# A decoder layer with 32 experts: experts of at most 64 tokens on unsplit float32 weights, one expert to a step

## Chip, core and metric

The kernel runs on one core of one Trainium2 chip. The metric is the device time of one execution in microseconds (us). Five engines work side by side, each through its own instructions in order: TensorE (PE, with PEld for its weight loads), VectorE (DVE), ScalarE (ACT), GpSimd (POOL) and SyncE (SP), which issues most transfers (DMAs).

## What is computed

The layer has 512 tokens of 1024 elements. Attention and a matrix memory come first; then each token goes to 4 of 32 experts. The change is in the experts alone:

```python
def expert_block(args):
    xb, eb = args
    up = jnp.dot(xb, w_up[eb]) + b_up[eb]              # 1024 -> 2048
    glu, lin = jnp.split(up, 2, axis=-1)
    glu = jnp.minimum(glu, SWIGLU_LIMIT)
    lin = jnp.clip(lin, -SWIGLU_LIMIT, SWIGLU_LIMIT)
    act = glu * jax.nn.sigmoid(SWIGLU_ALPHA * glu) * (lin + 1.0)
    return jnp.dot(act, w_down[eb]) + b_down[eb]       # 1024 -> 1024
```

Everything is float32. An expert's weights are 12 MB, so 384 MB are read for all of them.

## The kernel before

The first 440 us or so hold everything up to the routing. After that the experts run in steps. Weights come in tiles of 1 MB, [128, 2048] in SBUF: eight for an expert's up projection, four for its down projection, 384 in all. `rawtile` gives each the next of eight raw buffers (`NW`); `up_w` and `dn_w` issue its load on SP, which waits until that buffer is free.

`wsplit` makes two float32r tiles of a raw one: `whi`, the value rounded (an ACT copy, line 1111), and `wlo`, the rest (a DVE subtraction, line 1103). The tokens are split too (`tsplit`), and `mm_w` builds a product out of three: high by high, low by high, high by low. `parts` keeps four tiles ahead (`NS`): whichever tile PE works on, the splits of the next three already stand in the orders of ACT and DVE.

The experts are sorted by their number of tokens, and `KINDS` says what a step holds. S is one expert with up to 128 slots; a tile is 12 matmuls of 512 columns. X is the one with up to 192. H is a pair of experts with up to 64 slots each. In H, the stationary operand has the high parts of 64 tokens in one half of PE's columns and their low parts in the other, so that a tile is 8 matmuls; `low` copies the lower half of the result into the bias table `bt` and `comb` adds it to the upper half, with the bias.

A step's order is that of `tiles`: the up tiles of its expert with the down tiles of the step before in between. `after_tiles(n, f)` puts f behind the n-th tile that follows; the activation's transposes (`turn`), the gather's transposes (`turn_x`), the scatter of an expert's rows and the index computations (`prep`) are placed so. From step 2 on PE, ACT, DVE and POOL follow this order literally (`manual_schedule`). PSUM is four tiles: `uA` and `uB` for an up projection, `dn` for a down projection and `t` for all transposes.

Rows of tokens are gathered by an indirect DMA of POOL into the one buffer `xg0` (line 1117), and results scattered into `y4` in HBM (line 1296). After the last step the four rows of each token are loaded from `y4` (`partial`), weighted and summed on DVE, normalized and stored (`finish`). The last expert's result stays on chip and is added by matmuls (line 1672).

Of the kernel before, what the change touches and what calls it, by code (L numbers as in the profile page):

```python
# [9 lines left out]
F32 = mybir.dt.float32  # L10
# [29 lines left out]
SLOTS = {"S": (128,), "X": (192,), "H": (64, 64)}  # L40
KINDS = "SSHSSHSSHSXSHSSHSSHSHSHS"
# [3 lines left out]
def _steps():  # L45

    steps, caps = [], []
    for kd in KINDS:
        steps.append((SLOTS[kd], len(caps)))
        caps += SLOTS[kd]  # L50
    by = [*range(E0), *sorted(range(E0, E), key=lambda x: -caps[x])]
    assert len(caps) == E and KINDS.count("X") == 1 and KINDS[-1] == "S"
    return steps, [by.index(x) for x in range(E)], [caps[x] for x in by]
# [6 lines left out]
def _const_main():  # L60
# [7 lines left out]
    c[:, C_R:C_R + 32] = np.array(_steps()[1])[None]  # L68
# [52 lines left out]
def emit(tc, A, dbg=None, stop_at=99):  # L121
# [911 lines left out]


    bt = ep.tile([128, 3072], F32R, name="bt")
    sel = ep.tile([64, 2, 32], F32R, name="sel")
    for i in range(2):
        o = slice(32 * i, 32 * i + 32)
        nc.vector.tensor_copy(sel[o, 0], cst[o, C_ID + 32 * i:C_ID + 32 * i + 32])
    cmb = [ep.tile([128, 2, 64], F32R, name=f"cmb{i}") for i in range(2)]  # L1040
    for t in cmb:
        nc.vector.tensor_copy(t[64:128], cst[64:128, C_ID + 64:C_ID + 128][:, None, :].to_broadcast([64, 2, 64]))

    scat = []

    def bias_rows():
        up_, dn_ = A["b_up"][0], A["b_down"][0]
        for c, tg, src in ((0, "y", up_[:, 0:1024]), (1024, "l", up_[:, 1024:2048]), (2048, "y", dn_)):
            raw = ep.tile([64, 1024], F32, name=f"braw{c}", tag=tg)
            for r in (0, 32):  # L1050
                nc.gpsimd.dma_start(raw[r:r + 32], src)
            if c == 1024:
                nc.gpsimd.tensor_scalar(raw, raw, 1.0, 1.0, op0=OP.add, op1=OP.mult)
            o = bt[0:64, c:c + 1024]
            nc.scalar.activation(o, raw, AF.Copy)
            nc.gpsimd.tensor_tensor(o[32:64], raw[32:64], o[32:64].bitcast(F32), op=OP.subtract)

    def indices(sets, tag, late=False):
# [12 lines left out]

        def rest():
# [9 lines left out]
            return nc.vector.scalar_tensor_tensor(di, ti, 4.0, sv[:, :, 2], op0=OP.mult, op1=OP.add)  # L1082
        return ti, di, rest if late else rest()

    def half_w(src, c, k2):

        raw = rawtile([128, 2, 2, 512])
        for r in range(2):
            k.load(raw[:, r], src[(2 * k2 + r) * 128:(2 * k2 + r + 1) * 128, :].rearrange(
                "p (h c n) -> p h c n", h=2, c=2)[:, :, c, :])  # L1090
        return raw
# [6 lines left out]
    hold, los = [0], []  # L1098

    def lows():  # L1100
        while los and not hold[0]:
            lo, f, hi = los.pop(0)
            nc.vector.tensor_sub(lo, f, hi.bitcast(F32))  # L1103

    def wsplit(raw):

        nb[0] += 1
        f = raw if len(raw.shape) == 2 else raw.rearrange("p a n -> p (a n)") if len(raw.shape) == 3 else raw.rearrange(
            "p a b n -> p (a b n)")
# [14 lines left out]
    def tsplit(src, nm, kd=(128,), scale=None):  # L1124

# [3 lines left out]
        n = sum(kd)  # L1129
        pz = pq.tile([128, 8, n], F32, name=f"{nm}T{nb[0]}", tag="t")  # L1130
        for kk in range(KT):
            c = slice(kk * 128, (kk + 1) * 128) if nm == "x" else slice(kk // 2 * 256 + kk % 2, kk // 2 * 256 + kk % 2 + 255, 2)
            nc.tensor.transpose(pz[:, kk, :], src[:, c], ident[0:n, 0:n])  # L1133
        t = ep.tile([128, 8, 256], F32R, name=f"{nm}t{nb[0]}", tag=f"t{s_}")
        w = kd[0]
        v = t[:, :, 0:2 * n].rearrange("p k (e c s) -> p k e c s", c=2, s=w)
        if n == 2 * w:
            v = t.rearrange("p k (e c s) -> p (k e) c s", c=2, s=w)
            return t, k.split(v[:, :, 0], v[:, :, 1], pz.rearrange("p k (e s) -> p (k e) s", s=w), scale), s_
        return t, k.split(v[:, :, 0, 0], v[:, :, 0, 1], pz, scale), s_  # L1140
# [5 lines left out]
    def mm_w(outs, xT, kk, ws, first, j=None, last=False):  # L1146


        if j is not None:
            x = xT[0][:, kk, 128 * j:128 * j + 128]  # L1150
            for c in range(2):
                for o, w in zip(outs, ws):
                    nc.tensor.matmul(o, lhsT=x, rhs=w[c], start=first and c == 0, stop=last and c == 1)  # L1153
            return
# [8 lines left out]
    def mm_b(outs, sel_, c0):  # L1163
        for n, o in enumerate(outs):
            nc.tensor.matmul(o, lhsT=sel_.to_broadcast([64, 128]), rhs=bt[0:64, c0[n]:c0[n] + 512], start=False,
                             stop=True)

    def low(pt, c0):

        for h in range(2):  # L1170
            if c0[1] == c0[0] + 512:
# [39 lines left out]
    def etile(tag):  # L1211
        nb[0] += 1
        return ep.tile([128, D], F32, name=f"{tag}{nb[0]}", tag=tag)
# [532 lines left out]
```

## Time and profile before

| | us |
|---|---|
| median of 3 runs | 1611.37 (1611.22 to 1612.34) |
| the profiled execution's own time | 1610.24 |
| its span, first to last instruction | 1608.5 |
| PE busy | 1471.2 (91%) |
| DVE busy | 1351.0 (84%) |
| ACT busy | 1109.5 (69%) |
| POOL busy | 208.9 (13%) |
| bytes moved by DMA | 494.21 MB, mean 307 GB/s |

A share over the whole span mixes stages with different limits. In the profile's slices one digit is a fortieth of the span, 40.2 us. PE's busy time counts overlapping matmuls with modelled ends: how long PE needs for a matmul is read from the distance of two starts.

### The profile page before, as it was taken

Reading aid. Unit: us, or ns where it says so; the run is one execution under the profiler, and the core shown is the slowest. Engines: PE = TensorE matmul, PEld = TensorE weight load, DVE = VectorE, ACT = ScalarE, POOL = GpSimd, SP = SyncE. Lnnn points to the kernel's source line nnn. Section 1 sums busy time; section 2 is a strip of 40 time slices with the busy share of each in tenths; the row PEclk is TensorE's granted clock in tenths of the full one; section 3 lists DMA queues with packets and bytes.
Section 4 is the critical chain, followed back from the end, with each engine's and each line's share of the span. In section 5 each row is a group of like instructions: output and inputs, shape, how many; then the busy total and the mean of one; then the engine's idle time right before and its main releaser. Section 6 shows DMA issues by size and latency. Waiting matters only on the chain. (4 is left out here: it accounts for less than half of the span.)

```text
span 1608.5 us, 19732 instructions
## 1 busy us (share of the span) xinstructions
PE 1471.2 (91%) x6923; PEld 1121.7 (70%) x6923; DVE 1351.0 (84%) x1472; ACT 1109.5 (69%) x1071; POOL 208.9 (13%) x164
## 2 busy tenths in 40 slices
PE   7999999898679999999999999979999999999980
PEld 2888775676557678777777777758777777676760
DVE  2786737766878899999899676989999899999976
ACT  3555425564456888888698566958887888989951
POOL 0200100000450011021020010301022020110002
PEclk9999999999689999999999999989999999999995
DMA  8522257228387999999999777989999999999952
GB/s 293 168 70 79 67 173 263 101 89 303 136 320 286 344 419 408 404 404 420 367 415 402 298 294 276 395 331 379 372 415 418 351 413 403 420 419 418 417 241 97
DMA packets 104843, 494.21 MB, mean 307 GB/s; under 512 B 14330, under 2 KB 39395, under 8 KB 52643
## 3 DMA queue, kind: packets, MB, share of 16 engines
q1 hardware_dynamic: 96339, 472.12, 75.1%
q0 software_dynamic: 8400, 20.78, 3.6%
q8 instruction: 56, 0.92, 0.2%
q14 instruction: 48, 0.39, 0.1%
HBM read 474.77 MB, written 27.00 MB: 312 GB/s over the span
## 5 line engine op out<-in xcount | busy, mean ns | idle before, releaser
L1103 DVE TENSOR_TENSOR wlo<-raw,whi 128x2048 fp32r<-128x2048 f32 x384 | 861.2, 2294 | 51.4 <-ACT whi L1111 51.0
L1111 ACT ACTIVATE whi<-raw 128x2048 fp32r<-128x2048 f32 x384 | 719.0, 1911 | 80.0 <-PE dn L1153 28.0
L1117 POOL DMA_INDIRECT xg<-h2d,tis x25 | 70.1, 2806 | 571.4 <-PE xT L1133 563.5
L1296 POOL DMA_INDIRECT y<-y,dis x24 | 48.7, 2028 | 376.1 <-ACT y L1326 211.5
L1153 PE MATMUL ug<-wlo,xt 128*128 128x512 f32 x256 | 86.7, 420 | 10.8 <-DVE wlo L1103 7.1
L1153 PE MATMUL dn<-wlo,at 128*128 128x512 f32 x272 | 87.1, 401 | 1.8 <-DVE wlo L1103 1.4
L1153 PE MATMUL dn<-whi,at 128*128 128x512 f32 x272 | 88.4, 406 | 0.0
L1157 PE MATMUL dn<-whi,at 128*128 128x512 f32 x256 | 82.1, 402 | 1.2 <-ACT y L1335 1.2
L1153 PE MATMUL ug<-whi,xt 128*128 128x512 f32 x256 | 82.0, 401 | 1.3 <-ACT sg L1335 1.3
L1161 PE MATMUL dn<-wlo,at 128*128 128x512 f32 x256 | 81.9, 401 | 0.5
L1157 PE MATMUL ug<-whi,xt 128*128 128x512 f32 x240 | 80.4, 416 | 1.2 <-issue 1.2
L1159 PE MATMUL dn<-whi,at 128*128 128x512 f32 x256 | 80.9, 397 | 0.0
L1153 PE MATMUL ul<-whi,xt 128*128 128x512 f32 x256 | 80.4, 395 | 0.0
L1153 PE MATMUL ul<-wlo,xt 128*128 128x512 f32 x256 | 80.4, 395 | 0.0
L1157 PE MATMUL ul<-whi,xt 128*128 128x512 f32 x240 | 77.1, 403 | 1.6 <-DVE l L1208 1.5
L1159 PE MATMUL ul<-whi,xt 128*128 128x512 f32 x240 | 76.7, 400 | 0.0
L1159 PE MATMUL ug<-whi,xt 128*128 128x512 f32 x240 | 76.6, 401 | 0.0
L1161 PE MATMUL ug<-wlo,xt 128*128 128x512 f32 x240 | 76.0, 397 | 0.0
L1161 PE MATMUL ul<-wlo,xt 128*128 128x512 f32 x240 | 75.2, 394 | 0.0
L1153 PEld LDWEIGHTS ug<-wlo,xt 128*128 128x128 f32 x256 | 43.6, 189 | 42.2 <-DVE wlo L1103 36.1
L1153 PEld LDWEIGHTS dn<-wlo,at 128*128 128x128 f32 x272 | 50.9, 190 | 17.8 <-DVE wlo L1103 6.5
L113 ACT ACTIVATE xt<-xT 128x1024 fp32r<-128x1024 f32 (+1 forms) x25 | 25.3, 1011 | 53.4 <-PE xT L1133 53.4
(548 smaller groups left out, 2968.2 us busy)
## 6 DMA issues: line engine op xcount, KB each, us to landing
raw<-in_w_up_dram SPq DMA_DIRECT2D x247, 1024.0 KB, 8.3
raw<-in_w_down_dram SPq DMA_DIRECT2D x128, 1024.0 KB, 8.7
wada<-in_w_ada_dram SPq DMA_DIRECT2D x24, 1024.0 KB, 6.9
y<-zero SPq DMA_DIRECT2D x4, 2048.0 KB, 16.4
raw<-in_w_up_dram SPq DMA_DIRECT2D x16, 512.0 KB, 8.8
raw<-y SPq DMA_DIRECT2D x7, 1024.0 KB, 8.1
wor<-in_w_out_dram SPq DMA_DIRECT2D x4, 1024.0 KB, 6.1
x<-in_x_dram SPq DMA_DIRECT2D x8, 256.0 KB, 4.6
```

Of the source, the lines that this page charges most:

```text
L113: return (nc.scalar.activation(hi, src, AF.Copy), nc.vector.tensor_sub(lo, src, hi.bitcast(F32)))
L1103: nc.vector.tensor_sub(lo, f, hi.bitcast(F32))
L1111: nc.scalar.activation(hi, f, AF.Copy)
L1117: k.last = nc.gpsimd.indirect_dma_start(out=xg0[0:n], out_offset=None, in_=h2d, in_offset=bass.IndirectOffsetOnAxis(ap=ti[0:n], axis=0), b ...
L1153: nc.tensor.matmul(o, lhsT=x, rhs=w[c], start=first and c == 0, stop=last and c == 1)
L1157: nc.tensor.matmul(o, lhsT=xh, rhs=wh, start=first, stop=False)
L1159: nc.tensor.matmul(o, lhsT=xl, rhs=wh, start=False, stop=False)
L1161: nc.tensor.matmul(o, lhsT=xh, rhs=wl, start=False, stop=False)
L1296: st = nc.gpsimd.indirect_dma_start(out=y4, out_offset=bass.IndirectOffsetOnAxis(ap=di[0:n], axis=0), in_=ys, in_offset=None, bounds_check ...
```

## The change

- `KINDS` becomes `"SS" + "NS" * 3 + "NNXN" + "NS" * 10`. H is gone: each of its 16 experts is a step of its own, N, with up to 64 slots. There are 32 steps instead of 24, with the same 15 S and the one X, and the same slots by rank.
- An N expert's tokens are transposed and copied without a split (`tcopy`), and its weights are not split. Each tile takes four float32 matmuls with the raw tile as the moving operand: the same 64 tokens are loaded into the left and into the right half of PE's columns, the left half makes the outputs 0 to 511 and the right half 512 to 1023, each into its own 64 PSUM partitions. The X expert's tokens past 128 are treated so as well, beside the split tiles of its first 128.
- `low`, `comb`, `hold` and the delayed low splits are gone. The bias is the first matmul of the sum, with a selector `cm` of 128 columns.
- `bt` becomes [128, 3, 512], with the left halves' biases on 64 partitions and the right halves' on the others, made by one copy and two subtractions.
- The activation's `sg` is written in place in PSUM.
- An N expert's result is [128, 512]: 64 rows in two halves. It is scattered by half rows into `y4` with indices `dh`.
- A step's tiles stand in plain order: eight up tiles of its expert, then four down tiles of the step before.

```diff
-KINDS = "SSHSSHSSHSXSHSSHSSHSHSHS"
+KINDS = "SS" + "NS" * 3 + "NNXN" + "NS" * 10
...
-        nc.scalar.activation(hi, f, AF.Copy)
-        los.append((lo, f, hi))
-        lows()
+        k.split(hi, lo, f)
...
+    def tcopy(src, nm, scale=1.0):
+
+        nb[0] += 1
+        n, w = (8, 64) if nm == "x" else (4, 128)
+        pz = pq.tile([128, n, w], F32, name=f"{nm}N{nb[0]}", tag="t")
+        for kk in range(n):
...
+            nc.tensor.transpose(pz[:, kk, :], src[:, c], ident[0:w, 0:w])
+        t = ep.tile([128, n, w], F32, name=f"{nm}n{nb[0]}", tag=f"{nm}n")
+        nc.scalar.activation(t, pz, AF.Copy, scale=scale)
+        return t
...
+            if xn is not None:
+                for a in range(2):
+                    for c in range(2):
+                        o = a * 1024 + c * 512
+                        nc.tensor.matmul(self.pn[64 * c:64 * c + 64, a], lhsT=xn[:, kk, :], rhs=raw[:, o:o + 512],
+                                         start=False, stop=kk == KT - 1, skip_group_check=True)
...
+            if an is not None:
+                for b in range(2):
+                    for n in range(2):
+                        nc.tensor.matmul(self.pn[64 * n:64 * n + 64], lhsT=an[:, c % 2 * 2 + b, 64 * (c // 2):64 * (c // 2) + 64],
+                                         rhs=raw[:, b, 512 * n:512 * n + 512], start=False, stop=c == 3 and b == 1,
+                                         skip_group_check=True)
...
+            if an is not None:
+                yn = etile("yn", 512)
+                nc.scalar.activation(yn, self.pn, AF.Copy)
+                after_tiles(2, lambda: scatter(yn, self.dis[1]))
...
+        return [("u", kk) for kk in range(KT) if i < E] + [("d", c) for c in range(4) if i > 0]
...
-                ready.append(wsplit(raw))
+                raw = ahead.pop(0) if ahead else up_w(source(i)[0], x) if c == "u" else dn_w(source(i - 1)[1], x)
+                ready.append((raw, wsplit(raw) if KINDS[i - (c == "d")] != "N" else None))
```

PE, in one of the last steps. Before, the fourth up tile of an H expert, two down tiles of the S expert before it, and the first up tile of the pair's other expert (`whi`, `wlo` are a tile's split parts, `xt` and `at` the tokens and the activation, `cmb0` the selector of `comb`):

```order
L1153 MATMUL ug1191_11631<-whi1196_11691,xt1179_11500 128x512 x2
L1153 MATMUL ul1192_11632<-whi1196_11691,xt1179_11500 128x512 x2
L1153 MATMUL ug1191_11631<-wlo1196_11692,xt1179_11500 128x512 x2
L1153 MATMUL ul1192_11632<-wlo1196_11692,xt1179_11500 128x512 x2
L1157 MATMUL dn1201_11755<-whi1197_11705,at1186_11601 128x512 x2
...
L1179 MATMUL ul1192_11632<-bt_4277,cmb0_4281 64x512 x2
L1179 MATMUL ug1191_11631<-bt_4277,cmb0_4281 64x512 x2
...
L1153 MATMUL ug1204_11800<-whi1199_11736,xt1179_11500 128x512 x2
```

Now, an N expert's step: its bias and up tiles, then the first down tile of the S expert before it (`xn` is the unsplit tokens, `un` the N expert's PSUM tile):

```order
L1195 MATMUL un951_9713<-bt_4277,cm26_9706 128x512 x2
L1204 MATMUL un951_9713<-raw308_9674,xn947_9625 64x512 x4
L1204 MATMUL un951_9713<-raw309_9680,xn947_9625 64x512 x4
...
L1113 MATMUL xT953_9757<-cst_86,xg0_3887 128x128 x8
L1204 MATMUL un951_9713<-raw314_9735,xn947_9625 64x512 x4
L1204 MATMUL un951_9713<-raw315_9741,xn947_9625 64x512 x4
L1137 MATMUL dn958_9799<-whi952_9749,at949_9695 128x512 x2
```

Eight matmuls of a tile became four, which read the raw tile itself, and the bias stands first.

ACT, near the end of the experts. Before, every tile has its copy:

```order
L1111 ACTIVATE whi1230_12108<-raw374_12106 128x2048
L1172 ACTIVATE bt_4277<-dn1227_12069 64x1024
L1111 ACTIVATE whi1231_12123<-raw375_12121 128x2048
L1335 ACTIVATE y1232_12141<-dn1227_12069 64x1024
L1111 ACTIVATE whi1233_12145<-raw376_12143 128x2048
```

Now, from the last up tile of one S expert to its first down tile:

```order
L110 ACTIVATE whi994_10369<-raw351_10367 128x2048
L1126 ACTIVATE xn995_10418<-xN995_10409 128x512
L1173 ACTIVATE ug989_10291<-ug989_10291 128x1024
L111 ACTIVATE at997_10488<-aT997_10479 128x8x128
L1265 ACTIVATE yn998_10497<-dnn996_10458 128x512
L110 ACTIVATE whi1000_10542<-raw364_10540 128x2048
```

The raw tiles 352 to 363 no longer pass through ACT (nor DVE).

ACT, the last four tiles. Before, the last H pair's second result (`y`) is copied behind all of the last four splits, and behind its own `low` copy:

```order
L1111 ACTIVATE whi1239_12235<-raw381_12233 128x2048
L114 ACTIVATE at1240_12256<-aT1240_12247 128x8x128
L1111 ACTIVATE whi1241_12261<-raw382_12259 128x2048
L1172 ACTIVATE bt_4277<-dn1237_12210 64x1024
L1111 ACTIVATE whi1244_12304<-raw383_12302 128x2048
L1335 ACTIVATE y1232_12141<-dn1237_12210 64x1024
```

Now the last N expert's:

```order
L110 ACTIVATE whi1021_10838<-raw381_10836 128x2048
L111 ACTIVATE at1022_10855<-aT1022_10846 128x8x128
L110 ACTIVATE whi1023_10860<-raw382_10858 128x2048
L1265 ACTIVATE yn1024_10868<-dnn1019_10820 128x512
L110 ACTIVATE whi1027_10897<-raw383_10895 128x2048
```

The copy of the result moved ahead of the last split.

## Rows read from the trace of the kernel before

**Rows 1.** The page's first line, and its slices: the busy share of 40 slices of 40.2 us in tenths, and what the transfers moved.

```profile
span 1608.5 us, 19732 instructions
...
PE   7999999898679999999999999979999999999980
...
DVE  2786737766878899999899676989999899999976
...
DMA  8522257228387999999999777989999999999952
GB/s 293 168 70 79 67 173 263 101 89 303 136 320 286 344 419 408 404 404 420 367 415 402 298 294 276 395 331 379 372 415 418 351 413 403 420 419 418 417 241 97
```

**Rows 2.** Windows of the trace: stretch, its length, busy time of PE, PEld, DVE, ACT and POOL (with the number of instructions), granted TensorE clock, DMA share, GB/s.

```profile
529.00:1537.00 1008.00, 972.76 (x4277) 746.27 (x4276) 936.36 (x569) 814.58 (x517) 121.55 (x52) 0.99 0.96 383
880.00:1100.00 220.00, 203.47 (x893) 158.42 (x893) 176.98 (x145) 148.31 (x100) 26.94 (x11) 0.95 0.84 321
1380.00:1500.00 120.00, 117.29 (x501) 86.91 (x500) 119.28 (x67) 106.48 (x68) 12.62 (x5) 1.00 1.01 419
1530.00:1537.00 7.00, 7.00 (x30) 5.15 (x29) 6.90 (x5) 5.59 (x4) 0.00 (x0) 1.00 0.64 260
1537.00:1550.00 13.00, 9.04 (x40) 7.02 (x39) 10.57 (x6) 8.82 (x8) 2.67 (x1) 0.87 0.03 9
26.00:39.00 13.00, 10.74 (x77) 4.11 (x74) 0.05 (x1) 4.46 (x8) 0.00 (x0) 1.00 0.72 219
302.00:309.00 7.00, 6.72 (x18) 5.05 (x19) 4.61 (x14) 3.79 (x3) 0.00 (x0) 0.55 0.00 0
```

**Rows 3.** Waits of the DMA queue that SP issues, from 529 to 1537 us: who waited for whom, us in total, times, the longest.

```profile
SPq L947 <- DVE wlo L1103: 483.6, 214, 9.1
SPq L118 <- DVE wlo L1103: 276.5, 126, 9.5
```

**Rows 4.** Groups of DVE's instructions from 529 to 1537 us: line, operation, tiles, forms, count, then busy us and mean ns, then the idle time before them.

```profile
L1103 DVE TENSOR_TENSOR wlo<-raw,whi 128x2048 fp32r<-128x2048 f32 x357 | 797.0, 2286 | 40.1 <-ACT whi L1111 39.7
L1209 DVE SCALAR_TENSOR_TENSOR l<-sg,l 64x1024 f32<-64x1024 f32 (+1 forms) x29 | 35.5, 1223 | 3.7 <-ACT whi L1111 0.5 <-ACT sg L1207 0.4
L1208 DVE TENSOR_SCALAR l<-ul 64x1024 f32<-64x1024 f32 (+1 forms) x29 | 35.3, 1218 | 2.3 <-PE ul L1165 1.8 <-PE ul L1179 0.2
```

**Rows 5.** The same of ACT.

```profile
L1111 ACT ACTIVATE whi<-raw 128x2048 fp32r<-128x2048 f32 x358 | 669.6, 1911 | 57.6 <-PE dn L1153 28.0 <-PE u L1153 9.3 <-PE ul L1159 7.3
```

**Rows 6.** Timeline of PE near the end: start, us, engine, line, operation, tiles, forms, count. First eight transposes, then the split matmuls of an S expert.

```profile
1537.47 1.11 PE L1133 MATMUL aT<-cst,l 128*128 128x128 f32 x8
...
1550.25 0.63 PE L1157 MATMUL dn<-whi,at 128*128 128x512 f32 x2
...
1550.71 0.63 PE L1159 MATMUL dn<-whi,at 128*128 128x512 f32 x2
...
1551.18 0.63 PE L1161 MATMUL dn<-wlo,at 128*128 128x512 f32 x2
...
1551.65 0.63 PE L1157 MATMUL dn<-whi,at 128*128 128x512 f32 x2
```

**Rows 7.** Timeline of PE: the unsplit float32 matmuls of the modulation (stationary operand of 32 columns, four column quarters in turn), and two unsplit ones over all 128 columns.

```profile
32.82 3.64 PE L205 MATMUL ada<-wada,scT 128*32 128x512 f32 x32
...
90.17 1.12 PE L497 MATMUL rb<-rrow,cst 4*128 4x512 f32 x2
```

**Rows 8.** Timeline of SP around step 1: issues of weight loads (eight up tiles of step 2, then two of the down tiles after them).

```profile
494.19 23.27 SPq L947 DMA_DIRECT2D raw<-in_w_up_dram  x8
520.47 3.13 SPq L118 DMA_DIRECT2D raw<-in_w_down_dram  x2
```

**Rows 9.** Timeline of PE there: the bias matmuls that end step 1.

```profile
525.90 0.73 PE L1165 MATMUL dn<-bt,sel 64*128 64x512 f32 x2
```

**Rows 10.** PE's waits from 529 to 1537 us: us in total, times, the longest.

```profile
PE capr L1418 <- DVE capt L1416: 5.5, 1, 5.5
PE xT L1133 <- DVE svs L1080: 5.2, 2, 2.8
PE xrow L1449 <- DVE xtab L1438: 3.8, 1, 3.8
```

**Rows 11.** The page's DMA issues: transfer, queue, count, KB each, median us from issue to landing.

```profile
raw<-in_w_up_dram SPq DMA_DIRECT2D x247, 1024.0 KB, 8.3
```

**Rows 12.** Timeline of all engines in the tail: the last two low splits, the last down's first matmuls, the last H pair's scatter, the loads of y, the last bias matmuls.

```profile
1543.08 4.49 DVE L1103 TENSOR_TENSOR wlo<-raw,whi 128x2048 fp32r<-128x2048 f32 x2
...
1545.52 1.22 PE L1157 MATMUL dn<-whi,at 128*128 128x512 f32 x2 [1.18 <-ACT y L1335]
...
1545.74 2.67 POOL L1296 DMA_INDIRECT y<-y,dis  x1 [41.69 <-ACT y L1335]
...
1550.10 5.40 SPq L118 DMA_DIRECT2D raw<-y  x9
...
1558.74 0.72 PE L1165 MATMUL dn<-bt,sel 64*128 64x512 f32 x2
```

**Rows 13.** Timeline of PE while its granted clock was low: a wait, then matmuls of 512 columns.

```profile
302.28 0.45 PE L716 MATMUL Y<-ptl,V 128*128 128x384 f32 x1 [1.94 <-DVE ptl L113]
...
306.02 0.63 PE L96 MATMUL y<-woh,yTh 128*128 128x512 f32 x1
306.45 0.63 PE L97 MATMUL y<-wol,yTh 128*128 128x512 f32 x1
```

More of the change, by code (lines that the diff above doesn't have):

```diff
@@ L1081, in rest @@
             nc.vector.scalar_tensor_tensor(ti, sv[:, :, 0], float(OOB), sv[:, :, 1], op0=OP.add, op1=OP.add)
[L1082 to L1091, printed above, removed]
+            nc.vector.scalar_tensor_tensor(di, ti, 4.0, sv[:, :, 2], op0=OP.mult, op1=OP.add)
+            return nc.vector.tensor_scalar(dh, di, 2.0, half, op0=OP.mult, op1=OP.add)
+        return ti, di, dh, rest if late else rest()
+    half = rt.tile([128, 1], F32, name="half")
+    nc.vector.tensor_scalar(half, cst[:, C_P0:C_P0 + 1], 64.0, None, op0=OP.is_ge)
     def dn_w(src, c):
@@ L1144, in ptile, with mm_w @@
         return pq.tile([128, 2, 512], F32, name=f"{nm}{nb[0]}", tag=tag)
[L1146 to L1154, printed above, removed]
+    def mm_w(outs, xT, kk, ws, first):
         xh, xl = xT[0][:, kk, 0:128], xT[0][:, kk, 128:256]
@@ L1470, in prep @@
         for i in some:
-            kd, e = steps[i]
             p_, t_ = (posm, tab) if i < E0 else tb[2:]
-            if len(kd) > 1:
-                new = [[(p_[:, :, e + h], t_[:, :, :, e + h], sum(kd[:h]), sum(kd[:h + 1])) for h in range(len(kd))]]
-            else:
-                new = [[(p_[:, :, x], t_[:, :, :, e], 0, 128)] for x in ((e, 32) if kd[0] > 128 else (e,))]
-            sets += new
-            own += [i] * len(new)
-        ti, di, last = indices(sets, f"s{some[0]}", late)
@@ L1480, in prep @@
-        for n, i in enumerate(own):
-            idx.setdefault(i, []).append((ti[:, n:n + 1], di[:, n:n + 1]))
+            kd = KINDS[i]
+            if kd != "N":
+                sets.append([(p_[:, :, i], t_[:, :, :, i], 0, 128)])
+                own.append((i, 0))
+            if kd != "S":
+                sets.append([(p_[:, :, 32 if kd == "X" else i], t_[:, :, :, i], 64 * c, 64 * c + 64) for c in range(2)])
+                own.append((i, 1))
+        ti, di, dh, last = indices(sets, f"s{some[0]}", late)
@@ new lines, in emit, with turn_x @@
+        if gs:
+            xg = [gather(gs[0][1], (128, 64)[gs[0][0]])]
+        if kd == "N":
+            tags = tags[::-1]
+        up = Up(xT, sel_, cm, tags[0])
+        def turn_x():
+            b = gs[0][0]
+            if b == 0 and not free:
+                return False
+            nxt[b] = (tsplit, tcopy)[b](xg[0], "x")
+            gs.pop(0)
+            if gs:
+                xg[0] = gather(gs[0][1], 64)
+                after_tiles(4, turn_x)
+        for n, (c, x) in enumerate(tiles(i)):
@@ L1586, in emit @@
             tick()
-        if len(nx) > 1:
-            turn_x(1)
-        assert len(nxt) == len(nx)
+        assert not gs
         xT = nxt
-        if i + 1 < len(steps):
-            down = Down(up, kd, sel_, [di for _, di in idx[i]])
+        if i + 1 < E:
+            down = Down(up, [x and x[1] for x in idx[i]], tags[1])
     by_hand.close()
@@ L1658, in emit @@
     pys = []
-    down = Down(up, kd, sel_, [], pys.append)
-    for c, j, x in tiles(len(steps)):
-        down.tile(j, x, parts())
+    down = Down(up, [], None, pys.append)
+    for c, x in tiles(E):
+        down.tile(x, *parts())
     py = pys[0]
@@ L1665, in emit @@
         partial(q, yq[q])
-    yh, yl_ = (ep.tile([128, D], F32R, name=f"yr{t}", tag=t) for t in ("l", "sg"))
+    yr = ep.tile([128, 2, D], F32R, name="yr", tag=f"t{[x for x in free if x not in ysl][0]}")
+    yh, yl_ = yr[:, 0], yr[:, 1]
     k.split(yh, yl_, py)
```

364 lines of the change are left out of this document (136 added, 228 removed).

## Prediction

> **What bounds the kernel now.** I read the slices first [rows 1]. From the 14th slice on two rows stand near the top together: DVE at 8 or 9 and the DMA share at 9, except for a trough around slices 23 to 25. PE is at 9 too, but that row counts modelled, overlapping ends. So there are two candidates, and the windows separate them [rows 2]. In the good stretch, 1380 to 1500 us, the transfers run at 419 GB/s with a DMA share of 1.01: that is the ceiling that this trace shows. Over all of 529 to 1537 us, which is the expert work from the 29th weight tile to the last, they average 383. The worst part, 880 to 1100 us around the expert with 192 slots, has 321.
>
> What holds the transfers back below the ceiling is read from the queue that issues them [rows 3]: 340 of its waits, 760 us in all, end with a wlo split. A raw buffer comes free when DVE has taken the low part out of it, so DVE's pace is the transfers' pace. The groups of DVE in that stretch [rows 4] show how tight this is: 357 splits of 2.286 us are 797 us, the activation's two operations add 71, and DVE is busy 936 us of 1008 [rows 2]. ACT's half of the split is 1.911 us a tile [rows 5]. One megabyte at 419 GB/s takes 2.5 us, so DVE has 0.2 us a tile for all the rest. **The bound is DVE's split in the bad stretches and the transfers in the good ones.**
>
> **What the change does to each engine.** Sixteen of the 32 experts (now N) lose both splits: 192 tiles times 2.286 us, 439 us, off DVE and 192 times 1.911, 367 us, off ACT. The order shows it: ACT goes from one S split to the next with twelve raw buffers between them that it never touches. For a pair of one N and one S expert DVE then has 12 x 2.286 plus four operations of 1.2 us and two half ones, about 34 us; the transfers need 24 x 2.5 = 60. DVE and ACT cease to matter.
>
> PE for an S expert is not changed. Six matmuls of 512 columns start within 1.40 us, 0.233 each [rows 6]; 144 of them, six for biases and sixteen transposes (eight in 1.11 us [rows 6]) make 37.5 us, against 30 us of transfer.
>
> PE for an N expert has four unsplit float32 matmuls a tile, in two pairs on the two column halves, where H had eight at 0.233, 1.86 us. The trace of before has no 64-column float32 pair, but it has a near relative: the modulation matmuls, unsplit float32 of 512 columns on four column quarters. Thirty-two of them take 3.64 us, 0.455 for each set of four side by side [rows 7]. Taking a pair as such a set, a tile costs 0.91 us. The upper bound is that halves don't overlap: 4 x 0.455 = 1.82 us. I take 0.91, since quarters plainly run side by side. Twelve tiles, three bias matmuls and twelve small transposes: 13 us. The pair of experts is 51 us of PE against 60 of transfer, so **the transfers become the only bound** in steady state.
>
> Rows first, then the skill: two float32 matmuls at full width end 1.12 us after the first began [rows 7], which four passes of 512 columns each (4 x 0.233 each, 1.86 for both) would exceed. The Trainium skill, FP8 and Floating Point Precision, TensorE Precision Notes, says that true FP32 takes four passes; the trace disagrees. By that rule an N tile would be about 1.8 us and the PE's sum for a pair about 62 us.
>
> **Term 1, the steady stretch.** The same bytes at 419 instead of 383 GB/s: 1008 x (1 - 383/419) = 86.6 us less [rows 2]. Gathers and scatters carry the same rows; a half-row scatter moves the same bytes in twice the pieces.
>
> **Term 2, the start.** Steps 0 and 1 are S as before. The next eight tiles, issued from 494.19 us on, are step 2's [rows 8]. Before, their buffers came free with the split, four tiles ahead of PE, so the ninth issue was at 520.47. Now PE must read them, and it reaches them after step 1's bias matmuls, at 525.90 + 0.73 [rows 9], plus 0.9 for the tile: 527.5. The queue runs dry for 7 us: **+7**.
>
> **Term 3, what still stalls.** The X tile on PE is 12 x 0.233 + 0.91 = 3.7 us, eight of them 30 us against 20, and the overflow tables stop PE for 5.5 and 3.8 us, an index step for 2.8 [rows 10], each behind the splits that stand ahead on DVE. Eight raw buffers (20 us of transfers) take most of this, as a load lands 8.3 us after its issue [rows 11] and three in flight keep the queue busy. Between 0 and 25; I take **+10**, the size of the table's two stops.
>
> **Term 4, the tail.** Weights have landed at 1537 [rows 2]; the last splits run until 1547.57, the pair's last scatter goes out at 1545.74, the loads of y at 1550.10 and the last bias matmuls at 1558.74, that is 13 and 22 us after the landing [rows 12]. Now the last N expert's y is copied behind the third of the last four splits (ACT's order): about at the last landing. The scatter takes 2.67 us and lands 1.7 later, so y is loaded at about +4.5; the last down, which needs the same PSUM, runs 48 x 0.233 + 0.7 = 12 us. Both come 8 to 10 us sooner; **-9**, with 0 and -13 as ends.
>
> **Nothing for** the single table of biases (one copy and two subtractions of 1536 columns in place of three of each of 1024, once, beside step 0), the copies of the selector on POOL, and 8 more gathers and scatters: POOL is idle most of the stretch (122 us of 1008 [rows 2]). If that cover were gone, a late gather would stop PE at the transposes, some 2 us a step.
>
> **Sum**, on the profiled execution's own 1610.2 (span 1608.5 and 1.7 around it; the median of the runs is 1.1 above): 1610.2 - 86.6 + 7 + 10 - 9 = 1531.6, so **1532 us**.
>
> **Rival 1: PE's lag outgrows the raw buffers.** S work now stands in runs of twelve tiles (down of one S, up of the next, in two steps), 37.5 us of PE in 30 of transfer. N tiles no longer leave their buffers by a split, so PE's lag fills the ring. In the N run PE is busy 0.9 of 2.5 us, and its clock may fall: here it fell to half (0.55 in 302 to 309 us [rows 2], the 1.2 GHz level) after PE had stood waiting, and 512 columns then took 0.43 us [rows 13]. The Trainium skill, TensorE: Matmul & The Clock Gate, HAM oscillation, describes just that for matmul bursts that wait for loads; whether gaps of 1.6 us do it, no row shows. Lag of 7.5, 3 for a cold beginning and 3 for an index stop is 13.5 us, five tiles of the eight. Against: splits run four tiles ahead, which adds room. If it spills, 3 to 5 us in each of 13 pairs: 1571 to 1597. Chance 0.20.
>
> **Rival 2: the halves run one after the other**, at full clock: 1.82 us a tile, 62 us of PE a pair; 2 us each for 13 pairs and the stalls no longer hidden: 1560 to 1590. The four-pass rule gives the same time. Chance 0.06.
>
> **Rival 3, slower than before:** halves one after the other (or four passes) and half the clock through the N runs. A tile is then 3.6 us, above its transfer; an N expert takes 46 us, a pair 84 against 60, so 13 pairs lose over 300 us: about 1850. It begins to be slower than before where a pair takes 66 us, that is from 2.2 us a tile on. For it: N runs are exactly where PE idles. Against: the modulation matmuls, also paced by loads, ran at clock 1.00 [rows 2]. Chance 0.07.
>
> **Rival 4: nothing is gained**, since the ring, now released by PE in N steps, gives the same average of 383: 1600 to 1613. Against: 340 waits name the split. Chance 0.04.
>
> **How the numbers follow.** The forecast has 0.63: 1532, with 1506 to 1560 from the ends of terms 3 and 4 and a ceiling that may stand 1% higher. Adding rival 1 and most of rival 2 brings 8 in 10: 1506 to 1585. This kernel's runs can tell 0.2% from no change (3 us). Faster by more: 0.63 + 0.20 + 0.06 and a little of rival 4, 0.90; slower: rival 3, 0.07; the same: 0.03.
>
> **What would show it.** Right: DMA share about 1.0 from 530 us to the last weight, its queue waiting for PE in N steps, DVE near half busy, no split waits; N pairs 0.45 us apart; the last weight landing about 1465. Wrong: DMA share with regular dips once in two experts (rival 1), N matmuls of one pair starting 0.45 us apart instead of together (rival 2), a granted clock near half over the N runs (rivals 1 and 3).

## The result: a sixth of the forecast's gain

Five runs of the kernel after have a median of 1598.71 us (1595.38 to 1601.06), the kernel before 1612.34 beside it. The ratio is 0.9908, with an interval of 0.9887 to 0.9928: 13.6 us less where 79 were forecast, and outside the range. The profiled execution is the one of 1598.71; its span is 1596.7 (before 1608.5).

The slices of the kernel after answer to [rows 1]:

```profile
span 1596.7 us, 19183 instructions
...
PE   6999999998769999999797979999999999999990
...
DVE  1786737766888547363422165374572653744666
...
DMA  8522246318487899999967879999999999999962
GB/s 291 164 80 80 63 151 233 138 48 312 180 283 285 317 419 410 411 412 421 356 240 294 322 325 398 419 417 415 417 414 408 406 414 409 417 405 404 419 266 119
```

DVE fell to half and the transfers stand near their ceiling in most slices, as forecast. But from the 20th to the 24th they sag to 240 to 356 GB/s, as before: the trough around X is all there. Its first tile is earlier in the program now (at 785 us, before at 886), so the two kernels are cut at different places, about 57 us ahead of that tile in each. Windows, with the columns of [rows 2]; the middle row of each is the stretch around X. Before:

```profile
529.00:829.00 300.00, 290.58 (x1285) 222.91 (x1284) 284.15 (x160) 248.39 (x156) 32.89 (x16) 0.99 0.98 397
829.00:1129.00 300.00, 283.07 (x1257) 220.93 (x1256) 254.93 (x189) 213.38 (x141) 42.11 (x18) 0.97 0.88 344
1129.00:1526.00 397.00, 388.11 (x1695) 293.98 (x1694) 386.38 (x216) 344.21 (x217) 46.55 (x19) 1.00 1.00 405
```

After:

```profile
529.00:729.00 200.00, 197.12 (x937) 119.33 (x939) 106.15 (x77) 87.03 (x61) 22.98 (x18) 1.00 1.00 406
729.00:1029.00 300.00, 262.12 (x1176) 141.46 (x1174) 117.85 (x131) 93.05 (x72) 27.08 (x23) 0.94 0.86 342
1029.00:1521.00 492.00, 477.10 (x2206) 297.04 (x2203) 274.55 (x191) 227.02 (x156) 51.50 (x36) 1.00 1.01 412
```

From such rows I work out what a stretch loses against the 419 GB/s of [rows 2]: its length times (1 - rate/419). Before: 15.8 + 53.7 + 13.3 us; after: 6.2 + 55.1 + 8.2. **Outside X 29 us became 14. Around X 54 became 55.** All tables below use this measure.

Two smaller sums complete it. SP, the start of step 2 and the tail of the kernel after, beside [rows 8] and [rows 12]:

```profile
499.12 20.56 SPq L944 DMA_DIRECT2D raw<-in_w_up_dram  x8
530.89 3.76 SPq L115 DMA_DIRECT2D raw<-in_w_down_dram  x3
1516.64 4.74 SPq L115 DMA_DIRECT2D raw<-in_w_down_dram  x3
1536.84 2.43 POOL L1230 DMA_INDIRECT y<-yn,dhs  x1 [32.87 <-ACT yn L1265]
1540.73 5.47 SPq L115 DMA_DIRECT2D raw<-y  x9
```

The last weight loads of the kernel before:

```profile
1515.37 11.35 SPq L118 DMA_DIRECT2D raw<-in_w_down_dram  x6
```

The queue stops for 530.89 - 519.68 = 11.2 us at the start, where it stopped for 3.0: +8.2. From the last weight load's issue to the end of the span there were 1608.5 - 1526.7 = 81.8 us and are 1596.7 - 1521.4 = 75.3: -6.5. With -13.3 from the stretches that is -11.6; the span fell by 11.8. The agreement is closer than the measure: in bytes the start costs less, since from 430 to 529 us 261 GB/s went where 286 went before, 2.5 MB or 5.9 us at 419 GB/s.

What the queue of the loads waits for now (529 to 1524 us, beside [rows 3]):

```profile
SPq L944 <- PE dnn L1258: 234.2, 64, 15.8
SPq L944 <- DVE wlo L110: 189.2, 84, 9.5
SPq L115 <- PE un L1204: 122.3, 68, 11.1
SPq L944 <- PE un L1204: 107.3, 67, 6.3
SPq L115 <- DVE wlo L110: 106.1, 56, 8.2
```

N's buffers are freed by TensorE, S's by the split, as the forecast said. At the ceiling such a wait costs nothing: a load has to wait for some buffer.

And what PE waits for from 700 to 1010 us (total, times, longest):

```profile
PE dnn L1251 <- DVE ln L1175: 10.1, 2, 8.5
PE capr L1351 <- DVE capt L1349: 6.8, 1, 6.8
PE aN L1124 <- ACT xn L1126: 5.5, 1, 5.5
PE xrow L1382 <- DVE xtab L1371: 3.8, 1, 3.8
...
PE un L1195 <- ACT yn L1265: 3.1, 1, 3.1
```

That is 29 us in single stops; `dnn`, `xn` and `un` (18.7) are new. The granted clock over the middle window is 0.94 (0.97 before), which makes some 36 us at the 1.2 GHz level (an estimate, 300 x 0.06 x 2). No run takes that away by itself; it shrinks together with the stops (0.98 in f8_spread below).

**The price of an N tile.** PE's timeline: three down tiles, six up tiles, two up tiles, then the unsplit parts of three of X's up tiles:

```profile
1016.99 5.37 PE L1258 MATMUL dnn<-raw,an 128*64 128x512 f32 x24
...
1025.98 10.52 PE L1204 MATMUL un<-raw,xn 128*64 128x512 f32 x48
...
1037.45 3.65 PE L1204 MATMUL un<-raw,xn 128*64 128x512 f32 x16
...
789.20 1.94 PE L1204 MATMUL un<-raw,xn 128*64 128x512 f32 x8
...
794.08 1.94 PE L1204 MATMUL un<-raw,xn 128*64 128x512 f32 x8
...
798.95 1.94 PE L1204 MATMUL un<-raw,xn 128*64 128x512 f32 x8
```

A tile's four matmuls show as eight instructions, two for each: x48 is six tiles, in 10.52 us, x16 two, in 3.65, and X's part of one tile is x8. The page counts the up matmuls of 17 N parts with eight tiles as 1088 = 17 x 8 x 8, twice what the code writes. So an N tile costs about 1.75 us (10.52 over six), not 0.91, and X's tiles follow each other every 4.87 us, where a transfer takes 2.5.

### The profile page after: what moved, and what is told of

The parts are those of the page before. It is cut to its first block, busy times and chain, and to the rows that moved or that the text cites. A ratio compares the mean times of both kernels' runs of the same rounds, so it can differ in the third digit from the quotient of the medians.

```text
span 1596.7 us, 19183 instructions
## 1 busy us (share of the span) xinstructions
PE 1441.4 (90%) x7000; PEld 935.7 (59%) x7000; DVE 906.0 (57%) x1308; ACT 693.2 (43%) x838; POOL 186.4 (12%) x189
## 4 chain that ended last, share of the span: by engine, by line
PE 35%; DMA 18%; DVE 7%; issue 7%; ACT 3%; POOL 0%; ACTq 0%; DVEq 0%; POOLq 0%; SPq 0%
DMA raw<-in_w_down_dram 9%; DMA raw<-in_w_up_dram 9%; PE un L1204 8%; PE dnn L1258 6%; DVE wlo L110 4%; ACT whi L110 2%; PE ug L1137 2%; PE ul L1137 2%; PE ug L1139 2%; PE ug L1141 2%; PE ul L1141 2%; PE ul L1139 2%; PE dn L1141 1%; PE dn L1137 1%; PE dn L1139 1%
## 5 line engine op out<-in xcount | busy, mean ns | idle before, releaser
L110 DVE TENSOR_TENSOR wlo<-raw,whi 128x2048 fp32r<-128x2048 f32 x192 | 438.7, 2306 | 263.0 <-ACT whi L110 258.0
L110 ACT ACTIVATE whi<-raw 128x2048 fp32r<-128x2048 f32 x192 | 366.9, 1914 | 298.7 <-DMA raw<-in_w_down_dram 182.8
L1204 PE MATMUL un<-raw,xn 128*64 128x512 f32 x1088 | 243.5, 598 | 0.0
L1204 PEld LDWEIGHTS un<-raw,xn 128*64 128x64 f32 x1088 | 74.8, 137 | 144.7 <-issue 144.5
L1258 PE MATMUL dnn<-raw,an 128*64 128x512 f32 x544 | 126.5, 605 | 1.9 <-DMA raw<-in_w_down_dram 1.9
L1141 PE MATMUL dn<-wlo,at 128*128 128x512 f32 x256 | 83.9, 409 | 12.0 <-DVE wlo L110 12.0
L1137 PE MATMUL ug<-whi,xt 128*128 128x512 f32 x256 | 85.6, 416 | 1.4 <-issue 1.2
L1137 PE MATMUL dn<-whi,at 128*128 128x512 f32 x256 | 84.4, 411 | 2.2 <-ACT whi L110 1.6
L1141 PE MATMUL ug<-wlo,xt 128*128 128x512 f32 x256 | 82.8, 405 | 2.2 <-DVE wlo L110 2.2
L1141 PE MATMUL ul<-wlo,xt 128*128 128x512 f32 x256 | 82.0, 402 | 0.0
L1139 PE MATMUL ug<-whi,xt 128*128 128x512 f32 x256 | 81.8, 401 | 0.0
L1139 PE MATMUL dn<-whi,at 128*128 128x512 f32 x256 | 81.5, 400 | 0.0
## 6 DMA issues: line engine op xcount, KB each, us to landing
raw<-in_w_down_dram SPq DMA_DIRECT2D x128, 1024.0 KB, 13.3
```

What stands on the lines that cost most here:

```text
L110: return (nc.scalar.activation(hi, src, AF.Copy), nc.vector.tensor_sub(lo, src, hi.bitcast(F32)))
L1137: nc.tensor.matmul(o, lhsT=xh, rhs=wh, start=first, stop=False)
L1139: nc.tensor.matmul(o, lhsT=xl, rhs=wh, start=False, stop=False)
L1141: nc.tensor.matmul(o, lhsT=xh, rhs=wl, start=False, stop=False)
L1204: nc.tensor.matmul(self.pn[64 * c:64 * c + 64, a], lhsT=xn[:, kk, :], rhs=raw[:, o:o + 512], start=False, stop=kk == KT - 1, skip_group_ch ...
L1258: nc.tensor.matmul(self.pn[64 * n:64 * n + 64], lhsT=an[:, c % 2 * 2 + b, 64 * (c // 2):64 * (c // 2) + 64], rhs=raw[:, b, 512 * n:512 * n ...
```

## Experiments

Ratios are to the kernel before, run beside each on the same chip. "X" and "rest" are the lost us of the profiled execution, from windows cut as above (X is 829 to 1129 us in the order of before, 729 to 1029 in that of after; the rest ends with the last weight load). "Load to end" is the time from the first weight load that SP issues behind the routing to the end of the span. That issue, for the kernels before and after:

```profile
442.72 28.83 SPq L947 DMA_DIRECT2D raw<-in_w_up_dram  x8
...
445.93 25.81 SPq L944 DMA_DIRECT2D raw<-in_w_up_dram  x8
```

It comes between 441.7 and 447.4 us in these executions, 5.4 us apart in two kernels that do the same up to it (f4_all and f7_look), and a late one shows in the time and in "rest". The last column is free of it: three kernels of the same speed (after, e5_serial, e2_onecol) agree there within 3.3 us.

| kernel | us | ratio (interval) | X | rest | load to end |
|---|---|---|---|---|---|
| before | 1612.34 | 1 | 53.7 | 29.0 | 1165.8 |
| after | 1598.71 | 0.9908 (0.9887 to 0.9928) | 55.1 | 14.4 | 1150.8 |
| e1_half | 1580.31 | 0.9805 (0.9780 to 0.9831) | 38.7 | 11.2 | 1131.6 |
| e2_onecol | 1599.32 | 0.9915 (0.9887 to 0.9943) | 54.4 | 17.3 | 1153.9 |
| e5_serial | 1598.63 | 0.9918 (0.9895 to 0.9941) | 55.8 | 14.9 | 1150.6 |
| e6_before_nolow | 1574.55 | 0.9770 (0.9743 to 0.9797) | 40.8 | 5.6 | 1126.3 |
| e4_splitall | 1630.92 | 1.0124 (1.0097 to 1.0151) | 70.2 | 27.7 | 1184.5 |
| e3_xplain | 1557.94 | 0.9668 (0.9641 to 0.9696) | 12.9 | 12.8 | 1105.7 |
| f1_tag | 1588.80 | 0.9855 (0.9827 to 0.9883) | 42.2 | 14.9 | 1139.9 |
| f4_all | 1580.35 | 0.9802 (0.9776 to 0.9829) | 37.9 | 11.7 | 1132.4 |
| f7_look | 1575.91 | 0.9772 (0.9747 to 0.9796) | 32.2 | 15.5 | 1127.6 |
| f8_spread | 1572.45 | 0.9765 (0.9745 to 0.9785) | 28.6 | 14.1 | 1124.8 |
| g1_xhalf | 1562.76 | 0.9688 (0.9659 to 0.9717) | 18.6 | 17.3 | 1115.9 |
| f5_ring | 1583.53 | 0.9817 (0.9792 to 0.9842) | 40.8 | 12.3 | 1133.7 |
| f6_allring | 1580.13 | 0.9791 (0.9766 to 0.9816) | 37.9 | 14.2 | 1132.5 |
| f9_lookring | 1578.38 | 0.9804 (0.9781 to 0.9826) | 32.9 | 10.7 | 1128.8 |

### Is it TensorE's price of an N tile?

My first theory (A) was that the doubled N tile makes a pair of experts 62 us on PE, and that this is the new bound everywhere.

**e1_half**, N tiles at the forecast's price:

```diff
-                for a in range(2):
+                for a in range(1):
                     for c in range(2):
...
-                for b in range(2):
+                for b in range(1):
                     for n in range(2):
```

> The kernel after, in which an N tile takes two matmuls instead of four (the second half of each up tile's rows of outputs and the second of the two rows of each down tile are left out, also in X's part past 128 slots); every load stays. Theory A (each unsplit float32 matmul is two instructions of 0.43 us, an N tile 1.72 us, so that a pair of an N and an S expert is 62 us of TensorE and has no room to catch up): N tiles fall to 0.86 us, which is what the forecast had for whole ones; a pair outside the stretch around X takes 60.0 to 60.5 us instead of 63.2, X's stretch loses 15 to 30 of its 57 us because TensorE can catch up after it; 1530 to 1560 us. Theory B (the pairs are long since N steps free their raw buffers only when TensorE has read them, a matter of order and not of TensorE's work): the wait for TensorE stays at each N step, 1580 to 1600.

It gave 1580.31. The windows around X and behind it:

```profile
729.00:1029.00 300.00, 235.67 (x958) 136.79 (x959) 127.84 (x138) 101.47 (x79) 27.69 (x23) 0.85 0.92 365
1029.00:1501.00 472.00, 414.32 (x1791) 276.62 (x1790) 263.96 (x185) 217.66 (x150) 47.04 (x35) 0.92 1.00 412
```

Behind X the rate is 412 with half of N's matmuls and 412 with all of them. **Theory A falls there**: the transfers are the bound, and the doubled price costs nothing. Around X it costs 55.1 - 38.7 = 16 us, X's own second part included. B's range just holds the time, but not its reason: f5_ring below takes the rest of the stretch to 414 GB/s at most.

**e2_onecol**, one column half, and **e5_serial**, halves in another order:

```diff
-                    for c in range(2):
+                    for c in range(1):
```

> The kernel after with the right column half of all unsplit matmuls left out (outputs 512 to 1023 of N experts and of X's part past 128 slots): two matmuls a tile, each alone. Theory A (two halves run side by side): the time that TensorE needs for a tile stays at 4 x 0.43 = 1.72 us, and the whole at 1592 to 1602. Rival (the halves run one after the other, and four of them of one pass each make the 1.72): a tile falls to 0.86 us and the whole to that of the kernel with half of the matmuls, 1530 to 1560.

```diff
-                for a in range(2):
-                    for c in range(2):
+                for c in range(2):
+                    for a in range(2):
```

> The kernel after, with the four unsplit matmuls of a tile in another order: both of the left column half, then both of the right, instead of left and right in turn. If only neighbours on different halves run side by side: a tile takes 3 to 3.4 us on TensorE instead of 1.72, a pair of experts 78 to 82 instead of 62, and 13 pairs make it 1780 to 1850 us, slower than the kernel before (rival 3's end without its clock). If the halves run side by side whatever the order: 1595 to 1602.

Both run as the kernel after. PE's timeline of two up tiles, first e2_onecol's, which has half the instructions:

```profile
1038.43 3.65 PE L1204 MATMUL un<-raw,xn 128*64 128x512 f32 x8
```

then e5_serial's:

```profile
1038.45 3.70 PE L1204 MATMUL un<-raw,xn 128*64 128x512 f32 x16
```

Eight instructions on one half take as long as sixteen on both: the halves run side by side, and turns of left and right are not needed for it. Rival 2's and rival 3's first condition is excluded; 1.75 us is the price of two instructions for each float32 matmul.

### What is the splits' relief worth?

**e6_before_nolow**, the kernel before with DVE's relief alone:

```diff
-        los.append((lo, f, hi))
+        if low:
+            los.append((lo, f, hi))
+        else:
+            lo = hi
...
-                ready.append(wsplit(raw))
+                ready.append(wsplit(raw, KINDS[i - (c == "d")] != "H"))
```

> The kernel before, in which H tiles lose only VectorE's low split (the high part is used in its place, so that the low part of these weights is missing); matmuls, order and transfers are as before. The forecast's reading (VectorE's split paces the transfers, 192 x 2.286 = 439 us of it go): the mean rate from 529 us to the last weight rises from 383 to over 405 GB/s and the time falls by 40 us or more, to 1570 or less. Theory A (TensorE's work stood just below the transfers' before as well, and the waits for the low split were only the last of several near-equal ones): waits for the split turn into waits for the high split or TensorE, 1590 to 1612 us.

1574.55, 37 us less: between the two expectations, 5 us short of the forecast's reading. The windows:

```profile
529.00:829.00 300.00, 297.41 (x1353) 236.27 (x1352) 170.37 (x108) 262.47 (x165) 25.66 (x17) 1.00 1.01 416
829.00:1129.00 300.00, 291.14 (x1318) 229.10 (x1318) 173.57 (x157) 225.26 (x148) 23.02 (x17) 0.99 0.92 362
1129.00:1486.00 357.00, 348.92 (x1561) 274.60 (x1560) 180.93 (x114) 315.63 (x199) 25.05 (x18) 1.00 1.01 415
```

The forecast's reading of DVE is right outside X, where 29 lost us become 5.6, and theory A is wrong again. The mean rate stays under the 405 expected because of X: there DVE's relief brings 13 of 54: **41 us of that trough stay when the H tiles' low splits are gone.**

**e4_splitall**, the kernel after with the splits put back, unread:

```diff
-                ready.append((raw, wsplit(raw) if KINDS[i - (c == "d")] != "N" else None))
+                ready.append((raw, wsplit(raw)))
```

> The kernel after, with N tiles split all the same (ACT's copy and VectorE's subtraction of each, their results unread), so that only the relief of ScalarE and VectorE is taken back. Theory A' (outside X the stretch lost 26 us to the splits before and loses 12 now): the stretch outside X loses 15 to 30 us more and X's a little more, 1612 to 1640. Rival (what was gained came from the order and the tail, not from the splits): 1597 to 1605.

1630.92, as theory A' had it in size, though half of the extra loss stands around X (70.2 where 55.1 stood) and half outside. The missing splits are worth 32 us (1630.92 - 1598.71; 34 by the last column), and all else in the change costs 19 (1630.92 - 1611.80 of the kernel before beside it; 18.7 by the last column).

### What makes the trough?

**e3_xplain**, X without its tokens past 128:

```diff
-            if kd != "S":
+            if kd == "N":
                 sets.append([(p_[:, :, 32 if kd == "X" else i], t_[:, :, :, i], 64 * c, 64 * c + 64) for c in range(2)])
...
-        if kd != "S":
+        if kd == "N":
             cm = ep.tile([128, 2, 64], F32R, name=f"cm{i}", tag="cm", bufs=2)
```

> The kernel after with X's part past 128 slots left out (its gather, its matmuls, its activation and its scatter; those tokens' results are missing), so that X takes the path of an S expert. Theory C (the trough of the transfers from 760 to 960 us, 57 us long in sum, comes mostly from X: tiles of 4.87 us on TensorE and three waits in the order, for xn, un and dnn, of 5.5, 3.1 and 10.1 us): 1555 to 1575 us. Rival (the trough comes from the overflow tables and the low clock, X only happens to stand there): 1585 to 1600.

1557.94. X's stretch runs at 401 GB/s:

```profile
729.00:1029.00 300.00, 271.25 (x1262) 160.93 (x1261) 148.16 (x151) 116.57 (x85) 31.73 (x23) 0.96 0.98 401
```

Theory C holds: 42 of the 55 us are X's second part, its PE time and its stops together. The stops of the overflow tables are not among them: here too `capr` waits 6.1 us and `xrow` 3.8.

**f1_tag** and **f4_all** take single stops away:

```diff
-        down = Down(up, [x and x[1] for x in idx[i]], tags[1])
+        down = Down(up, [x and x[1] for x in idx[i]], tags[0])
```

> The kernel after with one change: X's down projection past 128 slots takes the other of the two PSUM tiles, so that it doesn't wait for the activation of the next N expert, which stands in VectorE's order behind splits of X's down tiles. What stood there is a wait of TensorE of 10.1 us and then 10 us at half the clock. Theory D (each stall in X's stretch is lost in full, since the transfers run at their ceiling before and after and can't catch up): 10 to 15 us less, 1583 to 1590. Rival (another wait in the order ends just as late, or the raw buffers take it): 1594 to 1602.

1588.80, in theory D's range: 9.9 us less than the kernel after (10.9 by the last column). Of the two stops of 10.1 us in sum the long one, 8.5, is gone and 1.6 stands.

```diff
-                after_tiles(4, turn_x)
+                after_tiles(3, turn_x)
...
-            if n == 3 and i == XS + 3:
+            if n == 1 and i == XS + 4:
                 selx, xrow = more(rank, xi)
```

> The PSUM change, and two moves in the order besides: the transposes of X's second gather one tile earlier, so that their copy stands in ScalarE's order ahead of the split of X's first tile, and the overflow tables ten tiles later, at an N expert's up tiles, where VectorE has no splits ahead of them. Theory D (stalls of 5.5, 10.1, 6.8 and 3.8 us, 26 in all, and part of the 37 us at half the clock that follow them): 25 to 40 us less, 1558 to 1575. Rival (X's tiles of 4.9 us on TensorE alone make the trough, and what is taken from the stalls is waited for elsewhere): 1580 to 1595.

This is on top of f1_tag's edit. 1580.35, 5 us above theory D's range and at the rival's lower end. Of the three waits aimed at (5.5, 6.8, 3.8), PE's timeline and waits show the first and second gone, `xrow` still there, and this in the first one's place:

```profile
779.44 1.19 PE L1195 MATMUL un<-bt,cm 128*128 128x512 f32 x2 [8.95 <-ACT yn L1265]
```

X's first matmul had waited 3.1 for the copy `yn`; with `xn` out of its way it waits 8.95. `yn` stands in ACT's order behind the high splits of X's first three tiles, and the first two of those wait for their loads. From ACT's timeline, the first of these splits and `yn`:

```profile
772.18 1.91 ACT L110 ACTIVATE whi<-raw 128x2048 fp32r<-128x2048 f32 x1 [7.12 <-DMA raw<-in_w_up_dram]
...
778.76 0.58 ACT L1265 ACTIVATE yn<-dnn 128x512 f32<-128x512 f32 x1
```

**f7_look** ends that, with the splits not ahead at that one place; **f8_spread** also parts the tables in two and spreads X's down tiles:

```diff
-        while plan and len(ready) < NS:
+        while plan and len(ready) < ns:
...
-            w = parts()
+            w = parts(min(4, 4 - x) if i == XS - 1 and c == "d" else NS)
```

> The kernel with the PSUM change and both moves, and in the step before X the splits no longer ahead of the last three down tiles: there ScalarE's copies of that expert's activation and result (an, yn) come ahead of the high splits of X's first three tiles, behind which TensorE waited 8.95 us, all engines idle but for the transfers. Theory D (X's stretch is a chain of single stalls, each lost in full): TensorE begins X at about 774 us instead of 779.4, and 4 to 8 us go, with less time at half the clock: 1571 to 1577 beside 1580 of the version without it. Rival (X's first tile waits for its own split anyway): 1578 to 1583.

1575.91: 4.4 us less than f4_all, in theory D's range. The two intervals overlap, so the time alone would not show it; but by the last column it is 4.8 us less, and the wait is gone:

```profile
778.61 0.71 PE L1195 MATMUL un<-bt,cm 128*128 128x512 f32 x2 [1.29 <-ACT yn L1265]
```

```diff
+        if i == XS + 1:
+            return [(c, int(x)) for c, x in zip("uuuuudududud", "012340516273")]
         return [("u", kk) for kk in range(KT) if i < E] + [("d", c) for c in range(4) if i > 0]
...
-            if n == 1 and i == XS + 4:
-                selx, xrow = more(rank, xi)
+            if n == 1 and i == XS + 4:
+                mo = more(rank, xi)
+                next(mo)
+            if n == 3 and i == XS + 4:
+                selx, xrow = next(mo)
```

> The same, and besides the overflow tables in two parts two tiles apart (a wait of 3.8 us), and X's four down tiles no longer in a row but one after each of the next N expert's last four up tiles, so that tiles of 4.6 us on TensorE alternate with tiles of 1.7 against a transfer of 2.6 each. Theory D with TensorE's lag: 4 us for the tables and 5 to 10 for the spread tiles: 1560 to 1571. If the raw buffers already cover X's down tiles: 1570 to 1576.

1572.45, just above the range; the last step of 3.5 us (2.8 by the last column) is within the spread of the runs. This version computes all of the reference and beats both kernels: 0.9765 of before. What is left around X, by **g1_xhalf**:

```diff
-                for a in range(2):
+                for a in range(1 if x else 2):
...
-                for b in range(2):
+                for b in range(1 if a else 2):
```

> The fastest version so far (1572 us: PSUM change, moves, tables in two parts, X's down tiles spread), in which X's tokens past 128 take two matmuls a tile instead of four (half of their sums is missing); N experts are whole. If what is left of X's stretch is TensorE's lag: X's up tiles fall from 4.87 to 4.0 us, and 8 x 0.86 = 7 us go, up to 10 with the down tiles: 1562 to 1566. If it is waits in the order: 1569 to 1574.

1562.76: 10 us less. f8_spread's row around X, then g1_xhalf's:

```profile
729.00:1029.00 300.00, 283.37 (x1287) 152.30 (x1284) 132.93 (x140) 108.21 (x82) 25.51 (x23) 0.98 0.94 379
```

```profile
729.00:1029.00 300.00, 284.08 (x1293) 156.42 (x1290) 140.67 (x143) 115.40 (x86) 32.18 (x26) 0.98 0.97 393
```

With the order mended, 12 x 0.87 us taken from PE give 10 us of time, as expected if PE's lag is what remains of X's second part. The 12.9 us that e3_xplain still loses around X are something else; no run isolates them.

**f5_ring**, **f6_allring** (on f4_all's order) and **f9_lookring** (on f7_look's, with the tables in two parts) have more raw buffers and splits one tile less ahead:

```diff
-NW = 8
-NS = 4
+NW = 10
+NS = 3
```

> The kernel after with 10 raw buffers in place of 8, and 3 pairs of split buffers in place of 4 with the splits 3 tiles ahead in place of 4. Rival B (N steps free buffers only when TensorE has read them, so the ring's depth sets the rate): the stretch outside X gains too, 1575 to 1590. Theory D (outside X the transfers are at their ceiling of 412 to 416 GB/s, and two more buffers cover 5 us of X's stretch once, as each stall there is covered by the same two): 1590 to 1597, with nothing outside 760 to 960 us.

> All of it together: the PSUM change, both moves in the order, and 10 raw buffers. Theory D: 30 to 45 us less than the kernel after, 1553 to 1570, the mean rate from 760 to 960 us at 370 GB/s or more instead of 306. If X's tiles on TensorE alone make the trough: 1575 to 1595.

> As the first of these three, with the overflow tables in two parts and 10 raw buffers in place of 8 (3 pairs of split buffers), X's down tiles in a row. Theory D: 4 us for the tables, and two more buffers cover 5 us of X's up tiles, now that no single stall uses them up: 1563 to 1572. If the ring of 3 split pairs costs as much as the raw buffers bring, as between the two versions of 1580 before: 1574 to 1581.

Alone, ten buffers bring 15 us. The size is rival B's, the place is theory D's: 14 of them around X (55.1 to 40.8), 2 elsewhere. Two buffers cover more of X than I gave them. On top of the mended order they bring nothing that can be told (1580.13 beside 1580.35, and 1578.38 where 1575.91 stood): both expectations of a further gain were misses, and the ranges of their rivals hold. That buffers and order cover the same stops is the likely reason, but not shown: the three pairs of split buffers, which f9_lookring's rival names, changed along with the raw buffers, and no run has the one without the other. Ten buffers together with spread down tiles were not tried.

## Why the prediction was wrong, point by point

- **Term 1 failed** ("the same bytes at 419 instead of 383 GB/s", -86.6). It took a mean over the whole stretch, and by its own row [rows 2] the 220 us around X at 321 GB/s are 220 x (1 - 321/419) = 51.5 of the 86.6. The bound "DVE's split in the bad stretches" was read for all of them at once from the wait totals [rows 3], and these name only the last link. From 829 to 1129 us the queue waits for `wlo` as elsewhere, but DVE's and ACT's groups in that window of the trace of before show what stood behind it:

```profile
L1103 DVE TENSOR_TENSOR wlo<-raw,whi 128x2048 fp32r<-128x2048 f32 x93 | 209.1, 2288 | 29.6 <-ACT whi L1111 29.5
...
L1111 ACT ACTIVATE whi<-raw 128x2048 fp32r<-128x2048 f32 x91 | 171.2, 1911 | 37.6 <-PE dn L1153 22.5 <-PE u L1153 9.3 <-PE ul L1159 3.5
```

  DVE's split stood idle for 29.6 us, nearly all of it behind ACT's, and ACT's for 37.6, nearly all of it behind TensorE's matmuls. In the two stretches outside X DVE's idle time is 5.9 and 4.6 us. So around X it was TensorE's lag that stood behind DVE's. e6 shows the low splits of H there worth 13 us of 54. Outside X the mechanism was right: 29 lost us became 14, and the last 8 of them come from a ceiling of 412 over 492 us, where I took 419 from 120.
- **Term 3 failed with it** (+10, "between 0 and 25"; 55 lost). X's tile was 4.87 us on PE, not 3.7, eight buffers did not "take most of this", and only the stops that the trace of before showed were counted. The change's own order brought three more. e3 shows 42 us for X's second part; f1, f4, f7 and f8 together take away 26 of the 55 by another order (the tables' stops among them), g1 another 10 by half of the second part's matmuls.
- **The N tile, 0.91 us, was wrong**: about 1.75. I read [rows 7], 32 rows in 3.64 us and two in 1.12, as one row to a matmul; it is two rows to one. The trace does not disagree, as the prediction had it, with what I set it against: the Trainium skill, FP8 and Floating Point Precision, TensorE Precision Notes, has true FP32 in four passes, and e2 shows 0.456 us (3.65/8) for each of the two instructions of a matmul on one half alone, 0.91 a matmul beside 4 x 0.233 = 0.93. Outside X this cost nothing (e1: 412 and 412 GB/s), around X 16 us. (The sum for an S expert, 37.5 us, comes to 37.2 from its own rows; nothing hangs on that.)
- **Term 2** (+7) measured +8.2 as a stop of the queue and +5.9 in bytes; **term 4** (-9) -6.5, where the same sum in the kernels of other runs with eight raw buffers and N steps is -4.2 to -8.8. Both are right in mechanism and nearly in size.
- **Nothing for the rest**: e4 shows +19 us for all but the splits. Its queue stops 11.2 us at the start too (+8.2) and its tail is 77.6 us (-4.2); the rest is X's stretch, which loses 70.2 where the kernel before, with the same splits, lost 53.7.
- **Rival 1** named the right place for lag, PE behind full raw buffers, but in every pair of experts; it happens once, at X. **Rival 2's** price of a tile was right by the four-pass rule; its result was not, since behind X the rate is 412 GB/s with these matmuls and with half of them (e1): a pair of about 61 us on PE (37.2 + 12 x 1.75 + some 2.4 for biases and transposes) does not hold back transfers of 24 x 1.0486 MB at 412 GB/s, 61 us too. **Rival 3** is excluded by e5 and by the clock of 1.00 behind X. **Rival 4**'s mean rate nearly came true (390 GB/s from 529 to 1521 us, from the three windows), but not by its mechanism: buffers freed by PE run at 412 outside X.

## What to carry to other kernels

Before a mean rate is turned into a gain, cut it where the mean is made, and ask in each piece which wait ends last there and what stood behind that wait: a trough with its own cause stays, whatever becomes of the rest. Where transfers run at their ceiling before and after, nothing makes up for a stop that the buffers don't cover (f1: 8.5 us of a stop, 9.9 us of time), so an order written by hand has to be read for what stands ahead of each small copy. And count the rows of one tile against the matmuls that the code writes before taking a price from them.

## What the runs showed of the hardware

- A float32 matmul of 512 columns is two instructions in the trace, 0.44 to 0.46 us each (10.52/24, 3.65/8) at the 2.4 GHz level (granted clock 1.00); two column halves of 64 run side by side, also when both matmuls of one half stand ahead of both of the other (3.70 us for two tiles, 3.65 in turns).
- With N's matmuls halved (e1), TensorE's granted clock fell once or more in each pair of experts: 0.92 in the mean behind X where it was 1.00, and about half (0.51, the 1.2 GHz level) in the window below, behind this wait on PE's timeline:

```profile
1210.08 0.73 PE L1137 MATMUL dn<-whi,at 128*128 128x512 f32 x2 [3.42 <-ACT whi L110]
```

  The Trainium skill, TensorE: Matmul & The Clock Gate, HAM oscillation, has matmuls that wait for loads lose the clock; the trace agrees. It cost nothing here, as the transfers stayed at 420 GB/s:

```profile
1211.00:1218.00 7.00, 5.88 (x15) 4.45 (x14) 6.31 (x4) 5.36 (x4) 0.00 (x0) 0.51 1.01 420
```
